# The MLP's two products by one level of Strassen's algorithm, with the hidden factors passing through DRAM

## The chip, the cores and the metric

One Trainium2 chip (trn2), one of its cores. The metric is device microseconds (us) for one execution of the whole program, lower is better. A core has a matrix engine (PE), which multiplies a stationary 128 x 128 block by a moving block of up to 512 columns into one of eight PSUM banks; a vector engine (DVE); a scalar engine (ACT); GpSimd (POOL); and a queue (SP) that issues DMAs. ACT issues DMAs as well. Every engine takes its instructions in the order in which they stand in its own queue.

## The reference

One layer of a hybrid block over 2048 latent tokens of width 1024 with 256 context tokens. The token mixer (Fourier mixing, a state-space layer and neighbourhood attention) is not touched here. What is touched is the second sub-layer:

```python
def sqrelu_mlp(h, w1, w2):
    return jnp.square(jax.nn.relu(h @ w1)) @ w2

h2 = modulate(rmsnorm(x, g_norm2[i]), sh2, sc2)
x = x + gt2 * sqrelu_mlp(h2, w_ff1[i], w_ff2[i])     # w_ff1 1024 x 4096, w_ff2 4096 x 1024
return rmsnorm(x, g_final)
```

## The kernel before, in words

The tail of the kernel is `merge_mlp`. It runs twice, over the tokens 1024 to 2047 and then 0 to 1023. Each half has three stages. `merged` makes the gated sum of the three branches. `projected` multiplies it by the output projection, adds the residual, and norms and transposes the result. `mlp` does the rest. Ahead of it stand the projections and the attention, which the change leaves as they are.

Every product is made to nearly float32 accuracy from factors that are each split in two float32r parts, high and low: `mm3` issues three matmuls (high by high, low by high, high by low; L176 to L178) for each pair of 128 x 128 and 128 x 512 blocks. A split is a copy on ACT (the high part, L169) and a subtraction on DVE (the low part, L173).

In `mlp`, 16 rounds each take two column blocks of 128 of the hidden layer. A round loads the weights, splits them, makes the hidden block for both blocks of 512 tokens (eight contraction blocks, 24 matmuls each), takes relu and square on ACT (L1366, L1367), splits the result, and multiplies by the rows of `w_ff2`. That is accumulated in SBUF: L1392 on DVE adds the PSUM bank into `x2`. The last round also norms and stores the output (L1394 to L1400). Over both halves there are 6144 matmuls of 512 columns.

All SBUF pages of these stages come from tagged rings: A1, X, W, R, T in one pool, A2, B1, B2 in another. A ring's next page waits for its earlier user. PSUM has banks g (2), t (2), s (3) and o (1). The program is written stage by stage, and a scheduler decides ahead of time how the instructions interleave on each engine; on the chip that order is fixed.

Of the kernel before, what the change touches and what calls it, by code (L numbers as in the profile page):

```python
# [20 lines left out]
P = 128  # L21
D = 1024
# [18 lines left out]
def constants():  # L41
    """Tables that depend on the shapes alone: DFT matrices and the column window."""
# [57 lines left out]
def block_kernel(ctx: ExitStack, tc: tile.TileContext, I, out, C, stages=None, taps=None):  # L100
# [32 lines left out]
    cd = dram.tile([8, P, 2, 2, P], F32, name="cd")  # L133
    scratch = dict(ud=ud, zd=zd, qd=qd, kd=kd, vd=vd, gd=gd, fad=fad, sbd=sbd, ncd=ncd, rid=rid)
# [10 lines left out]
    # ------------------------------------------------------------------ vectors  # L145
# [20 lines left out]
    # ------------------------------------------------------------------ helpers  # L166
# [8 lines left out]
    def mm3(out_, lh, ll, rh, rl, first, last):  # L175
        nc.tensor.matmul(out_, lh, rh, start=first, stop=False)  # L176
        nc.tensor.matmul(out_, lh, rl, start=False, stop=False)  # L177
        nc.tensor.matmul(out_, ll, rh, start=False, stop=last)  # L178
# [27 lines left out]
    # ------------------------------------------------------------------ modulation, first part  # L206
# [22 lines left out]
    def modulation(m1, c):  # L229
        """shift and scale of column tile c, for x and ctx"""  # L230
# [32 lines left out]
    # ------------------------------------------------------------------ phase A: u f k v q  # L263
# [14 lines left out]
    def products(wh, wl, blocks, kouter):  # L278
        """the blocks of tokens and their products with a unit of weights"""
# [67 lines left out]
    def gate(n, hx, half, kouter=False):  # L347
        """gd holds tanh(logit / 2)"""
# [6 lines left out]
    with pool("pa", side="right") as pa:  # L355
# [41 lines left out]
        # ------------------------------------------------------------------ modulation, second part  # L397
# [30 lines left out]
        # ---- relative-position tables: rows of rpd hold the bias at qc - kc + 63, 64 copies each, so that  # L428
        # a step of a row less one entry is a step of kc
# [37 lines left out]
    # ---- gated linear unit; sbd holds 4 * sb  # L467
# [143 lines left out]
def exp_dve(nc, sb, x, out, tag):  # L611
    """out = exp(x), to float32 accuracy; x is [P, n] and is overwritten."""
# [20 lines left out]
def sincos_dve(nc, sb, x, sn, cs):  # L633
    """sn, cs = sin(x), cos(x); x is [P, n] and is overwritten."""
# [24 lines left out]
    # odd quadrants exchange sine and cosine  # L659
# [12 lines left out]
def cmul(v, tmp, ore, oim, ar, ai, br, bi):  # L672
    """(ore, oim) = a * b, elementwise; the outputs may not be the inputs."""
# [8 lines left out]
def cmul_neg(v, tmp, ore, oim, ar, ai, br, nbi):  # L682
    """(ore, -oim) = a * b, for nbi = -im(b)."""
# [8 lines left out]
def s5_prep(g):  # L692
    """What depends on the parameters alone, into DRAM: lmd, ld (driving), kmd (chunk), cd (read-out).
    Three parts, so that other work can be placed between them."""
# [3 lines left out]
    with pool("s5") as sp:  # L698
        # ---- parameters: states (g2, p) on partitions, (direction, pair) along the free axis
# [4 lines left out]
        with pool("s5p") as pp:  # L704
# [27 lines left out]
            # (lbar - 1) / lam  # L732
# [18 lines left out]
            # powers of lbar, 0..8  # L751
# [6 lines left out]
            # powers of lbar**8, 1..16  # L758
# [9 lines left out]
            # bbar  # L768
# [6 lines left out]
            # c with states on partitions  # L775
# [22 lines left out]
        with pool("s5x") as sx:  # L798
# [9 lines left out]
            # X = lbar**i * bbar, in the order of the powers that the driving products need  # L808
# [9 lines left out]
            # read-out, rows (re, -im) of the states  # L818
# [46 lines left out]
def s5(g):  # L865
# [5 lines left out]
    with pool("s5", side="right") as sp:  # L871
# [4 lines left out]
        def load_u(sp, a, n):  # L876
            """the tokens of pairs a..a+n: (t, c) on partitions, (pair, h) and chunks along the free axis"""
# [12 lines left out]
        # ---- driving term of every chunk of 8 tokens  # L890
        with pool("s5x", side="right") as sx, pool("s5k", side="right") as sk:
# [21 lines left out]
            # ---- products within a chunk: both directions and the skip  # L913
# [63 lines left out]
        # ---- read-out  # L977
# [50 lines left out]
def attention(g):  # L1028
# [6 lines left out]
    with pool("at", side="right") as at:  # L1035
# [4 lines left out]
        def table(h):  # L1040
# [7 lines left out]
            # rows 4..28 see their own window of rows alone  # L1048
# [24 lines left out]
        def rows_of(a, q):  # L1073
            """query rows of quarter q that see a key row of tile a: all are contiguous"""
# [140 lines left out]
def merge_mlp(g):  # L1215
# [3 lines left out]
    G = 2  # L1219
# [7 lines left out]
    def small(shape=(P, NB), dt=F32):  # L1227
        return page("T", shape, dt)
# [9 lines left out]
    def branches(t0, b, br):  # L1238
        """the branches' outputs, transposed; the attention's rows are divided by their sums here"""
# [22 lines left out]
    def merged(t0, br):  # L1262
        """gated merge, transposed: m[d, tokens]"""
        parts = ((0, 2, "w_br_a"), (2, 4, "w_br_b"), (4, 8, "w_br_c"))
        mp, got = {}, {}
        for d, b in [(0, 0), (1, 0), (0, 1), (1, 1)] + [(d, b) for d in range(2, KT) for b in range(2)]:
# [15 lines left out]
            for i, (k0, k1, _) in enumerate(parts):  # L1282
# [4 lines left out]
                if i == 1:  # L1287
                    # the tokens of the second branch are in the order (t, c) for c * 8 + t
# [14 lines left out]
    def projected(t0, mp):  # L1303
        """output projection and residual, tokens on partitions; then the second norm"""
        x2, h2 = [], {}
        for n in range(2):
# [12 lines left out]
            for a in range(8):  # L1319
# [10 lines left out]
                if n == 1 and a % 4 == 3:  # L1330
                    b = a // 4
                    tiles = []
                    for aa in range(4 * b, 4 * b + 4):
                        r = rms(x2[aa])
                        xn = page("B1", (P, D), F32)
                        v.tensor_scalar(xn, x2[aa], r, None, op0=OP.mult)
                        tiles.append(xn)
                    for k in range(KT):
                        pt = psum("t")
                        for i, t in enumerate(tiles):  # L1340
                            nc.tensor.transpose(pt[:, i * P:(i + 1) * P], t[:, k * P:(k + 1) * P], ident)
                        tmp = small()
                        nc.scalar.activation(tmp, pt, AF.Identity, scale=g.a2[:, k:k + 1], bias=g.b2[:, k:k + 1])
                        p = page("A2" if b else "A1")
                        v.tensor_copy(p[:, 0], tmp)
                        v.tensor_tensor(p[:, 1], tmp, f32(p)[:, 0], op=OP.subtract)
                        h2[b, k] = p
        return x2, h2

    def mlp(t0, x2, h2, ahead):  # L1350
        """the MLP, the residual and the final norm; ahead() is placed before the last products"""
        for f0 in range(0, FF // P, G):
            hid, w2s = [], []
            for f in range(f0, f0 + G):
                raw = page("R", (P, KT, P), F32)
                nc.sync.dma_start(raw, I["w_ff1"][0, :, f * P:(f + 1) * P].rearrange("(k p) c -> p k c", p=P))
                wh = page("W", (P, KT, P))
                wl = page("W", (P, KT, P))
                g.splitw(raw, wh, wl)
                hb = []  # L1360
                for b in range(2):
                    pt = psum("g")
                    for k in range(KT):
# [79 lines left out]
```

## Time and profile before

| | |
|---|---|
| median of 3 runs | 3287.97 us (3285.66 to 3290.91) |
| span of the profiled execution | 3297.3 us |
| PE busy | 3182.4 us, 97% of the span |
| PE weight loads (beside the matmuls) | 78% |
| DVE, ACT, POOL busy | 59%, 36%, 20% |
| first `mlp` stage | about 1674 to 2395 us |
| second `mlp` stage | about 2577 to 3288 us |

The profiled execution is 9.3 us longer than the median. Matmuls are pipelined: the duration of one (0.39 us) is not what it adds to the time; the spacing of their starts is.

### The profile page before, as it was taken

How to read it: one execution, taken by the hardware profiler on the slowest of the kernel's cores; microseconds unless marked ns; L12 is line 12 of the kernel's file. 1: busy time of each engine (PE TensorE's matmuls, PEld its weight loads, DVE VectorE, ACT ScalarE, POOL GpSimd, SP SyncE). 2: the span in 40 equal slices, each digit the busy share in tenths (PEclk: the TensorE clock that was granted, in tenths of full speed). 3: DMA queues.
4: the chain of work that ended last, by engine and by line, in shares of the span. 5: the costliest groups of instructions: out<-in, count | busy, mean ns of one | idle time of the engine just before them, and what ended most of it. 6: DMA issues, size and time to landing. Idle time of an engine off the chain costs nothing.

```text
span 3297.3 us, 40319 instructions
## 1 busy us (share of the span) xinstructions
PE 3182.4 (97%) x14742; PEld 2585.7 (78%) x14742; DVE 1956.6 (59%) x3466; ACT 1185.8 (36%) x2153; POOL 664.9 (20%) x709
## 2 busy tenths in 40 slices
PE   8999787999999999999999999999999999999998
PEld 4887666788887788887788888888877888888887
DVE  6534379965888888847554444444575544444444
ACT  4242143364665556532232222222422322222222
POOL 0510124202565655524100000000151000000000
PEclk9999888999999999999999999999999999999999
DMA  6668863465436443266311111111473111111111
GB/s 207 200 202 247 207 164 98 140 190 174 115 114 207 115 119 111 84 184 193 118 39 51 51 52 51 40 50 45 121 255 108 40 45 51 52 52 49 41 48 61
DMA packets 394173, 370.26 MB, mean 112 GB/s; under 512 B 90688, under 2 KB 308943, under 8 KB 393591
## 3 DMA queue, kind: packets, MB, share of 16 engines
q1 hardware_dynamic: 310150, 294.80, 30.7%
q10 hardware_dynamic: 83248, 71.97, 7.1%
q8 instruction: 116, 1.90, 0.2%
q0 software_dynamic: 576, 0.92, 0.1%
q14 instruction: 83, 0.67, 0.1%
HBM read 282.79 MB, written 89.01 MB: 113 GB/s over the span
## 4 chain that ended last, share of the span: by engine, by line
PE 73%; DVE 6%; DMA 4%; ACT 0%; issue 0%; SPq 0%; POOL 0%; ACTq 0%; DVEq 0%; POOLq 0%
PE ps_g L176 13%; PE ps_g L177 13%; PE ps_g L178 13%; PE ps_s L178 5%; PE ps_s L176 5%; PE ps_s L177 5%; PE ps_t L176 4%; PE ps_t L178 4%; PE ps_t L177 4%; PE ps_s L1107 3%; PE ps_o L1160 1%; PE ps_o L1159 1%; PE ps_o L1163 1%; DMA pgR<-in_w_out_dram 1%; DVE Sx L975 1%; DVE tq L974 1%
## 5 line engine op out<-in xcount | busy, mean ns | idle before, releaser
L176 PE MATMUL ps_g<-pgA,pgW 128*128 128x512 f32 x1088 | 429.8, 395 | 2.4 <-DVE pgX L1292 1.5
L177 PE MATMUL ps_g<-pgA,pgW 128*128 128x512 f32 x1088 | 428.4, 394 | 0.0
L178 PE MATMUL ps_g<-pgA,pgW 128*128 128x512 f32 x1088 | 427.6, 393 | 0.0
L176 PE MATMUL ps_g<-hxh,whi 128*128 128x512 f32 x1024 | 408.0, 399 | 11.6 <-ACT ev L352 6.2
L178 PE MATMUL ps_g<-hxh,wlo 128*128 128x512 f32 x1024 | 406.4, 397 | 0.0
L177 PE MATMUL ps_g<-hxl,whi 128*128 128x512 f32 x1024 | 405.9, 396 | 0.0
L1392 DVE TENSOR_TENSOR pgX<-ps_t,pgX 128x512 f32<-128x512 f32 x256 | 176.1, 688 | 283.8 <-PE ps_t L178 283.7
L1235 POOL TENSOR_TENSOR st<-st,half_neg 128x1 f32<-128x1 f32 x32 | 22.2, 695 | 1573.4 <-DVE st L1234 1573.4
L1157 POOL TENSOR_TENSOR pl<-st,ph 128x512 fp32r<-128x512 f32 (+7 forms) x256 | 269.9, 1069 | 166.0 <-ACT ph L1155 154.7
L169 ACT ACTIVATE pgB<-pgR 128x1024 fp32r<-128x1024 f32 x64 | 68.0, 1063 | 647.1 <-PE ps_t L177 625.8
L176 PEld LDWEIGHTS ps_g<-pgA,pgW 128*128 128x128 f32 x1088 | 204.1, 188 | 49.9 <-DVE pgX L1292 1.9
L173 DVE TENSOR_TENSOR pgW<-pgR,pgW 128x1024 fp32r<-128x1024 f32 x80 | 106.9, 1336 | 228.4 <-ACT pgW L169 228.2
L178 PEld LDWEIGHTS ps_g<-pgA,pgW 128*128 128x128 f32 x1088 | 204.1, 188 | 47.8
L177 PEld LDWEIGHTS ps_g<-pgA,pgW 128*128 128x128 f32 x1088 | 204.1, 188 | 46.5
L176 PEld LDWEIGHTS ps_g<-hxh,whi 128*128 128x128 f32 x1024 | 195.5, 191 | 53.0 <-ACT ev L352 7.4
L177 PEld LDWEIGHTS ps_g<-hxl,whi 128*128 128x128 f32 x1024 | 195.6, 191 | 38.7 <-issue 0.5
L178 PEld LDWEIGHTS ps_g<-hxh,wlo 128*128 128x128 f32 x1024 | 195.3, 191 | 37.9
L1392 DVE TENSOR_TENSOR pgX<-ps_s,pgX 128x512 f32<-128x512 f32 x256 | 176.0, 688 | 68.1 <-PE ps_s L178 67.9
L178 PE MATMUL ps_t<-pgB,pgB 128*128 128x512 f32 x512 | 200.3, 391 | 0.0
L178 PE MATMUL ps_s<-pgB,pgB 128*128 128x512 f32 x512 | 200.2, 391 | 0.0
L176 PE MATMUL ps_t<-pgB,pgB 128*128 128x512 f32 x512 | 200.1, 391 | 0.0
L177 PE MATMUL ps_t<-pgB,pgB 128*128 128x512 f32 x512 | 199.8, 390 | 0.0
(439 smaller groups left out, 6828.8 us busy)
## 6 DMA issues: line engine op xcount, KB each, us to landing
pgR<-in_w_ff_dram SPq DMA_DIRECT2D x128, 512.0 KB
wraw<-in_w_in_dram SPq DMA_DIRECT2D x80, 512.0 KB
gd<-ev ACTq DMA_DIRECT2D x96, 256.0 KB
pgX<-gd SPq DMA_DIRECT2D x48, 512.0 KB
wm<-in_w_mod_dram SPq DMA_DIRECT2D x64, 256.0 KB
qs<-qd SPq DMA_DIRECT2D x128, 128.0 KB
wm<-in_w_mod_dram SPq DMA_DIRECT2D x16, 512.0 KB
xt<-in_x_dram SPq DMA_DIRECT2D x16, 512.0 KB
```

The source lines that it names most:

```text
L169: nc.scalar.activation(hi, raw, AF.Copy)
L173: e.tensor_tensor(lo, raw, f32(hi), op=OP.subtract)
L176: nc.tensor.matmul(out_, lh, rh, start=first, stop=False)
L177: nc.tensor.matmul(out_, lh, rl, start=False, stop=False)
L178: nc.tensor.matmul(out_, ll, rh, start=False, stop=last)
L974: v.tensor_tensor(tq, lm[l][:, h], car[c][:, h], op=OP.mult)
L975: v.tensor_tensor(dst[o][:, h], dst[o][:, h], tq, op=op)
L1107: nc.tensor.matmul(o, kk[:, j * P:(j + 1) * P], qs[:, i, p0:p1], start=i == 0, stop=i == 1)
L1157: e.tensor_tensor(pl[:, c0:c1], st[:, c0:c1], f32(ph)[:, c0:c1], op=OP.subtract)
L1159: nc.tensor.matmul(po[0:65, p0:p1], vh[:, j], ph[:, p0:p1], start=n == 0, stop=False)
L1160: last = nc.tensor.matmul(po[0:64, p0:p1], vl[:, j], ph[:, p0:p1], start=False, stop=False)
L1392: v.tensor_tensor(x2[a][:, cs], pt, x2[a][:, cs], op=OP.add)
```

## The change

One level of Strassen's algorithm (the form with seven block products and shared sums) replaces both products of the MLP. Each factor is cut into 2 x 2 blocks; seven products of sums and differences of blocks stand in for eight. Three PSUM accumulators are used per product (`CHAIN`): a bank is read after one block product and then accumulated on by the next.

The stages are taken apart. `projected` now also makes the seven token factors (28 splits, `factor`, and 4 kinds of differences, half of them on POOL) and stores the residual to DRAM (`x2d`). `hidden` makes all hidden blocks: 16 blocks q of 256 hidden columns, each of seven products of 12 matmuls. `prepare(q)` loads `w_ff1` (2 x 512 KB on SP) and makes four sums and differences on DVE (L1397 to L1400). `finish` (L1407 to L1435) takes the blocks out of PSUM, applies relu and square, makes three sums and differences on POOL that the second product will need, and writes seven float32 factors to DRAM (`hcd`) with five DMAs. `mlp` then reads them back: four quarters q, each of seven products of 48 matmuls over four banks, with both factors split anew; a quarter loads 8 x 512 KB of `w_ff2` and 14 x 512 KB of `hcd`. The result lies in eight SBUF pages `y`, and the gate `gt2`, the residual (read back from `x2d`) and the final norm come at the very end, where before `gt2` had been multiplied into the weights. Over both halves there are 5376 matmuls of 512 columns.

```diff
+    x2d = dram.tile([2, KT, P, D], F32, name="x2d")
+    hcd = [dram.tile([7, 16, P, NB], F32, name=f"hcd{t}") for t in range(2)]
...
+        def factor(j, k, src, tag):
+            p = page(tag)
+            nc.scalar.activation(p[:, 0], src, AF.Copy)
+            v.tensor_tensor(p[:, 1], src, f32(p)[:, 0], op=OP.subtract)
+            TW[j, k] = p
...
+                        if b == 0:
+                            factor(0, kk, blk[0, kk][:, 0], "A1")
+                            factor(1, kk, blk[0, kk][:, 1], "A1")
+                        else:
+                            t1, t2 = small(), small()
+                            nc.gpsimd.tensor_tensor(t1, blk[1, kk][:, 0], blk[0, kk][:, 0], op=OP.subtract)
+                            v.tensor_tensor(t2, blk[1, kk][:, 1], t1, op=OP.subtract)
+                            factor(2, kk, t2, "A2")
+                            factor(3, kk, t1, "A2")
+        for kk in range(4):
+            t1, t2 = small(), small()
+            nc.gpsimd.tensor_tensor(t1, blk[1, kk][:, 1], blk[1, kk][:, 0], op=OP.subtract)
+            factor(4, kk, t1, "B1")
+            factor(5, kk, blk[1, kk][:, 1], "B1")
+            nc.gpsimd.tensor_tensor(t2, blk[0, kk][:, 1], blk[0, kk][:, 0], op=OP.subtract)
+            nc.gpsimd.tensor_tensor(t2, t2, t1, op=OP.subtract)
+            factor(6, kk, t2, "B2")
...
+    CHAIN = ((0, True), (1, True), (0, False), (2, True), (0, False), (2, False), (0, False))
+    def hidden(t0, TW):
...
...
+        for q, j in steps:
+            if j == 0:
+                srcs[q], bank[q], cs[q] = prepare(q), {}, {}
+            b, new = CHAIN[j]
+            p = page("W", (P, 2, 4, P))
+            nc.scalar.activation(p[:, 0], srcs[q][j], AF.Copy)
+            v.tensor_tensor(p[:, 1], srcs[q][j], f32(p)[:, 0], op=OP.subtract)
+            if new:
+                bank[q][b] = psum("sgt"[b])
+            pt = bank[q][b]
+            for k in range(4):
+                t = TW[j, k]
+                mm3(pt, p[:, 0, k], p[:, 1, k], t[:, 0], t[:, 1], new and k == 0, k == 3, not new)
+            finish(q, j, pt, cs[q])
...
+    def mlp(t0, ahead):
+        for q in range(4):
...
+            for j in range(7):
+                L = split(hs, "B1")
+                R = split(src[j], "A2")
+                    for k in range(4):
+                        for i in range(4):
+                            product(i, k)
+                    for i in range(4):
+                        evict(i)
+                if last and j >= 5:
+                    for a in range(4 * (j - 5), 4 * (j - 4)):
+                        nc.sync.dma_start(xr, g.x2d[t0 // HALF, a])
+                        v.tensor_tensor(y[a], y[a], gt2, op=OP.mult)
+                        v.tensor_tensor(y[a], y[a], xr, op=OP.add)
+                        r = rms(y[a])
+                        v.scalar_tensor_tensor(y[a], y[a], r, gf, op0=OP.mult, op1=OP.mult)
+                        nc.scalar.dma_start(out[0, t0 + a * P:t0 + (a + 1) * P, :], y[a])
```

Up to the end of the first `projected` every engine's queue holds the same instructions in the same order as before. From there the queues differ. Three places follow.

The first is POOL's queue at the end of the first `projected`. Before, the four reciprocal roots of the last four token tiles (L1235) are all that stands there until the end of the half:

```order
L1235 TENSOR_TENSOR st_16871<-st_16871,half_neg_91 128x1
L1235 TENSOR_TENSOR st_16878<-st_16878,half_neg_91 128x1
L1235 TENSOR_TENSOR st_16885<-st_16885,half_neg_91 128x1
L1235 TENSOR_TENSOR st_16892<-st_16892,half_neg_91 128x1
L1235 TENSOR_TENSOR st_21429<-st_21429,half_neg_91 128x1
```

Now the sixteen differences of the token factors stand behind them, four of L1362 and then these twelve (pgT are the differences, pgB2 the transposed token blocks; the first of L1426 is already the hidden stage's):

```order
L1368 TENSOR_TENSOR pgT_16997<-pgB2_16905 128x512
L1371 TENSOR_TENSOR pgT_16998<-pgB2_16693 128x512
L1368 TENSOR_TENSOR pgT_17011<-pgB2_16928 128x512
L1371 TENSOR_TENSOR pgT_17012<-pgB2_16712 128x512
L1368 TENSOR_TENSOR pgT_17025<-pgB2_16951 128x512
L1372 TENSOR_TENSOR pgT_16998<-pgT_16998,pgT_16997 128x512
L1371 TENSOR_TENSOR pgT_17026<-pgB2_16731 128x512
L1368 TENSOR_TENSOR pgT_17039<-pgB2_16974 128x512
L1372 TENSOR_TENSOR pgT_17012<-pgT_17012,pgT_17011 128x512
L1371 TENSOR_TENSOR pgT_17040<-pgB2_16750 128x512
L1372 TENSOR_TENSOR pgT_17026<-pgT_17026,pgT_17025 128x512
L1372 TENSOR_TENSOR pgT_17040<-pgT_17040,pgT_17039 128x512
```

POOL had nothing of this size there; now it has a queue of sixteen operations of 128 x 512, the last of which makes the last part of the seventh token factor (`pgT_17040`).

The second is DVE's queue at the same place, from the split that reads that last difference on (pgW are the split weights; 17149 and 17166 are those of the products j = 2 and j = 3 of the first block, the fifth and sixth products that PE's queue holds):

```order
L1313 TENSOR_TENSOR pgB2_17050<-pgT_17040,pgB2_17050 128x512
L1398 TENSOR_TENSOR pgB2_17057<-pgB2_17057,pgX_17053 128x512
L1398 TENSOR_TENSOR pgB2_17105<-pgB2_17105,pgX_17101 128x512
L1400 TENSOR_TENSOR pgB2_17058<-pgX_17055,pgB2_17057 128x512
L1400 TENSOR_TENSOR pgB2_17106<-pgX_17103,pgB2_17105 128x512
L1448 TENSOR_TENSOR pgW_17149<-pgB2_17057,pgW_17149 128x512
L1448 TENSOR_TENSOR pgW_17166<-pgB2_17057,pgW_17166 128x512
```

Before, the casts and subtractions of the transposed tokens (L1345, L1346) stood between the split weights of that place. Now the weights of the fifth product to run stand behind the split of the seventh token factor.

The third is DVE's queue at the end of the program. Before, a residual add (L1392) and a final scaling (L1399) alternate:

```order
L1399 SCALAR_TENSOR_TENSOR pgX_22394<-pgX_22394,st_27404,pgB1_27316 128x1024
L1392 TENSOR_TENSOR pgX_22422<-ps_t_27418,pgX_22422 128x512
L1392 TENSOR_TENSOR pgX_22450<-ps_t_27441,pgX_22450 128x512
L1392 TENSOR_TENSOR pgX_22506<-ps_s_27479,pgX_22506 128x512
L1234 TENSOR_SCALAR st_27427<-st_27427 128x1
```

Now each of the eight pages passes DVE three more times (L1546 gate, L1547 residual, L1549 scaling), all of it behind the sixth of the last quarter's seven products. This is where the last pages' sums (L1529) stand:

```order
L1546 TENSOR_TENSOR pgX_25615<-pgX_25615,gt2_15527 128x1024
L1236 TENSOR_SCALAR st_27741<-st_27741 128x1
L1529 TENSOR_TENSOR pgX_25617<-ps_s_27291,pgX_25617 128x512
L1547 TENSOR_TENSOR pgX_25614<-pgX_25614,pgB2_27758 128x1024
L1549 SCALAR_TENSOR_TENSOR pgX_25611<-pgX_25611,st_27730,pgR_27267 128x1024
L1546 TENSOR_TENSOR pgX_25616<-pgX_25616,gt2_15527 128x1024
L1529 TENSOR_TENSOR pgX_25618<-ps_o_27292,pgX_25618 128x512
```

The gate and the residual moved from the weights and from the start value of the sum to a chain at the end.

## Rows read from the trace of the kernel before

**Rows 1.** The page's head: the span, and the busy time of each engine.
```profile
span 3297.3 us, 40319 instructions
PE 3182.4 (97%) x14742; PEld 2585.7 (78%) x14742; DVE 1956.6 (59%) x3466; ACT 1185.8 (36%) x2153; POOL 664.9 (20%) x709
```

**Rows 2.** Busy us of each engine (instructions) by stretch, granted clock, DMA share, GB/s.
```profile
core 0: us, PE busy (x) PEld busy (x) DVE busy (x) ACT busy (x) POOL busy (x), PEclk, DMA share, GB/s
1800.00:1900.00 100.00, 100.00 (x437) 81.66 (x437) 46.45 (x60) 22.75 (x32) 0.00 (x0) 1.00 0.14 42
2400.00:2500.00 100.00, 93.06 (x391) 73.51 (x390) 78.23 (x94) 25.25 (x37) 48.95 (x32) 0.98 0.71 234
```

**Rows 3.** PE's timeline around the end of the first projection: start, duration, what.
```profile
1674.07 0.40 PE L178 MATMUL ps_s<-pgA,pgB 128*128 128x512 f32 x1
1674.31 0.39 PE L176 MATMUL ps_g<-pgA,pgW 128*128 128x512 f32 x1
1675.00 1.04 PE L1341 MATMUL ps_t<-ident,pgB 128*128 128x128 f32 x8
```

**Rows 4.** As rows 2, the hand-over to the MLP and the program's end.
```profile
1674.00:1690.00 16.00, 15.71 (x90) 12.95 (x89) 12.18 (x24) 10.15 (x15) 0.55 (x1) 1.00 0.11 33
3287.70:3297.30 9.60, 0.00 (x0) 0.00 (x0) 5.08 (x7) 1.75 (x4) 2.06 (x3) 0.61 0.55 218
```

**Rows 5.** As rows 2, between the two halves.
```profile
2390.00:2416.00 26.00, 19.41 (x73) 14.24 (x72) 20.87 (x30) 6.53 (x10) 8.72 (x7) 0.93 0.96 330
2409.00:2412.00 3.00, 3.00 (x8) 2.40 (x9) 2.30 (x4) 1.27 (x2) 1.45 (x1) 0.53 1.02 408
```

**Rows 6.** ACT's timeline: evictions of the last transposed tokens.
```profile
1681.19 3.11 ACT L1343 ACTIVATE pgT<-ps_t,b,a 128x512 f32<-128x512 f32 x4 [3.06 <-PE ps_t L1341]
```

**Rows 7.** POOL's element-wise operations by source line: shortest, median and longest ns.
```profile
L1294 POOL TENSOR_TENSOR pgX<-pgX x64: 1274/1610/2284, 1497.0 to 2490.7; 128x512 f32<-128x512 f32 x64
L1397 POOL TENSOR_TENSOR pgX<-pgX,pgB x4: 2400/2632/3319, 2372.0 to 2385.1; 128x1024 f32<-128x1024 f32 x4
```

**Rows 8.** DVE's groups in the first MLP: count, busy us, mean ns, idle before.
```profile
L1392 DVE TENSOR_TENSOR pgX<-ps_t,pgX 128x512 f32<-128x512 f32 x126 | 86.7, 688 | 141.5 <-PE ps_t L178 141.5
L173 DVE TENSOR_TENSOR pgB<-pgT,pgB 128x512 fp32r<-128x512 f32 x64 | 44.1, 690 | 39.0 <-ACT pgB L169 38.9
L173 DVE TENSOR_TENSOR pgB<-pgR,pgB 128x1024 fp32r<-128x1024 f32 x32 | 39.1, 1220 | 17.8 <-ACT pgB L169 17.8
```

**Rows 9.** ACT's groups in the first MLP, columns as in rows 8.
```profile
L169 ACT ACTIVATE pgB<-pgT 128x512 fp32r<-128x512 f32 x63 | 39.6, 631 | 1.5
L1366 ACT ACTIVATE pgT<-ps_g 128x512 f32<-128x512 f32 x62 | 36.5, 591 | 77.2 <-PE ps_g L178 77.2
L169 ACT ACTIVATE pgB<-pgR 128x1024 fp32r<-128x1024 f32 x29 | 30.8, 1063 | 321.1 <-PE ps_t L177 312.9 <-DVE pgR L1374 8.1
```

**Rows 10.** ACT's issue of an output DMA, by source line, ns as in rows 7.
```profile
L1400 ACTq DMA_DIRECT2D out_dram<-pgX x16: 338/338/361, 2375.4 to 3293.4; - x16
```

**Rows 11.** DVE's timeline while POOL works.
```profile
2414.33 2.35 DVE L173 TENSOR_TENSOR pgW<-pgR,pgW 128x1024 fp32r<-128x1024 f32 x1 [0.17 <-ACT pgW L169]
2417.80 0.67 DVE L1292 SCALAR_TENSOR_TENSOR pgX<-pgX,ps_t 128x512 f32<-128x512 f32 x1
```

**Rows 12.** POOL's timeline at the same time.
```profile
2414.31 1.29 POOL L1294 TENSOR_TENSOR pgX<-pgX 128x512 f32<-128x512 f32 x1 [3.86 <-DVE pgX L1292]
2417.36 6.04 POOL L1294 TENSOR_TENSOR pgX<-pgX 128x512 f32<-128x512 f32 x4 [1.76 <-DVE pgX L1290]
```

**Rows 13.** The final scaling, group in columns as in rows 8.
```profile
L1399 DVE SCALAR_TENSOR_TENSOR pgX<-pgX,st,pgB 128x1024 f32<-128x1024 f32 x12 | 15.3, 1279 | 1.5 <-POOL st L1235 1.4
```

**Rows 14.** The chain that ended last, in order of time: a load, a store.
```profile
1551.52 5.80 DMA pgR<-in_w_out_dram
2400.40 7.65 DMA out_dram<-pgX
```

**Rows 15.** The same chain at the program's end.
```profile
3290.87 1.28 DVE pgX L1399
3292.15 1.20 DVEq L1439
```

More of the change, by code (lines that the diff above doesn't have):

```diff
@@ L173, in splitw, with mm3 @@
         e.tensor_tensor(lo, raw, f32(hi), op=OP.subtract)
[L175 to L178, printed above, removed]
+    def mm3(out_, lh, ll, rh, rl, first, last, more=False):
+        nc.tensor.matmul(out_, lh, rh, start=first, stop=False, skip_group_check=more)
+        nc.tensor.matmul(out_, lh, rl, start=False, stop=False, skip_group_check=more)
+        nc.tensor.matmul(out_, ll, rh, start=False, stop=last, skip_group_check=more)
     def rms_tile(sb, xt, n):
@@ L1303, in projected @@
     def projected(t0, mp):
-        x2, h2 = [], {}
+        x2, TW, blk = [], {}, {}
+        def factor(j, k, src, tag):
[3 more added lines that the diff above has]
+            TW[j, k] = p
         for n in range(2):
@@ L1336, in projected @@
                         v.tensor_scalar(xn, x2[aa], r, None, op0=OP.mult)
+                        nc.scalar.dma_start(g.x2d[t0 // HALF, aa], x2[aa])
                         tiles.append(xn)
[L1338 to L1363, printed above, removed]
-                        mm3(pt, wh[:, k], wl[:, k], h2[b, k][:, 0], h2[b, k][:, 1], k == 0, k == KT - 1)
-                    r = small()
-                    nc.scalar.activation(r, pt, AF.Relu)
-                    nc.scalar.activation(r, r, AF.Square)
-                    p = page("B1")
-                    g.splitw(r, p[:, 0], p[:, 1])
-                    hb.append(p)
-                hid.append(hb)
-                raw = page("R", (P, D), F32)
-                nc.sync.dma_start(raw, I["w_ff2"][0, f * P:(f + 1) * P, :])
-                v.tensor_tensor(raw, raw, gt2, op=OP.mult)
-                vh = page("B2", (P, D))
-                vl = page("B2", (P, D))
-                g.splitw(raw, vh, vl)
-                w2s.append((vh, vl))
-            last = f0 + G == FF // P
@@ new lines, in projected @@
+        for kk in range(4):
+            t1, t2 = small(), small()
[5 more added lines that the diff above has]
+            factor(6, kk, t2, "B2")
+        return TW
+    ORDER = (0, 1, 2, 3, 4, 5, 6)
+    CHAIN = ((0, True), (1, True), (0, False), (2, True), (0, False), (2, False), (0, False))
@@ new lines, in mlp, with split @@
+    def mlp(t0, ahead):
+        hcd = g.hcd[t0 // HALF]
+        y = [page("X", (P, D), F32) for _ in range(8)]
+        halves = [slice(n * NB, (n + 1) * NB) for n in range(2)]
+        def split(src, tag):
+            out = []
+            for s in src:
+                h, l = page(tag), page(tag)
+                nc.scalar.activation(h, s, AF.Copy)
+                v.tensor_tensor(l, s, f32(h), op=OP.subtract)
+                out.append((h, l))
+            return out
+        for q in range(4):
+            w = {}
+            for kk, n in ((0, 0), (1, 0), (0, 1), (1, 1)):
+                w[kk, n] = []
+                for h in range(2):
+                    r = page("A1", dt=F32)
+                    f0 = (8 * q + 4 * h) * P
+                    nc.sync.dma_start(r, I["w_ff2"][0, f0:f0 + 4 * P, halves[n]].rearrange(
+                        "(a k p) c -> k p a c", k=2, p=P)[kk])
+                    w[kk, n].append(r)
+            src = {0: w[0, 0], 1: w[1, 0]}
+            last = q == 3
@@ L1380, in mlp @@
             if last:
[L1381 removed]
+                gf = page("R", (P, D), F32)
                 nc.sync.dma_start(gf, bap(I["g_final"], 0, [[0, P], [1, D]]))
[L1383 to L1400 removed]
+            bank = {}
@@ L1415, in merge_mlp @@
         mp = merged(t0, br)
-        x2, h2 = projected(t0, mp)
-        mlp(t0, x2, h2, f)
+        hidden(t0, projected(t0, mp))
+        mlp(t0, f)
 _INS = ["x", "c", "ctx", "c_ctx", "w_mod", "b_mod", "g_norm1", "g_norm2", "w_in", "w_br_a", "w_br_b", "w_br_c",
```

119 lines of the change are left out of this document (100 added, 19 removed).

## Prediction

> **What bounds the kernel now.** I read the page's head first [rows 1]: PE is busy for 97% of the span, no other engine for more than 59%. Then the busy time by stretch [rows 2]. Inside an MLP stage PE is full, the granted clock is at its upper level (2.4 GHz), and 437 matmuls start in 100 us: one per 0.2288 us. That spacing, not the 0.40 us of a single record [rows 3], is the price of a matmul. The DMA share in the same row is 0.14 (42 GB/s), so memory has room. ACT's idle time in this stage ends on PE's matmul [rows 9], and so does DVE's at its residual add [rows 8]. So in the MLP PE is the limit, and fewer matmuls save time, as long as the other engines keep up with the new order. The two places where PE pauses today are the change of halves and the end [rows 4, 5].
>
> **What is removed.** 6144 matmuls become 5376, all of 128 x 512. 768 x 0.2288 = **175.7 us**. That is the only gain. All the rest of the change is new work on DVE, ACT, POOL and DMA, and I ask of each stage whether it hides behind PE.
>
> **A. From projection to hidden stage, twice.** Before, PE stays busy here: 15.71 of 16.00 us, in the first row of [rows 4]. Now the token factors stand between. The last projection matmul starts at 1674.07 [rows 3], and the queues are the same up to there. Behind it PE has 40 transposes, 1.04 us for eight [rows 3], 5.2 us in all, and the 48 matmuls of the hidden stage's first four products, 11.0 us. It runs dry at about 1690.3. The fifth product needs a split weight (`pgW_17149`) that DVE's queue holds behind the split of POOL's last difference. So POOL sets the time.
>
> POOL's first difference needs a second evicted block: ACT evicts from 1681.19, 0.78 us each [rows 6], so it starts at 1682.8. The next three follow as ACT goes on, which now evicts two blocks (2 x 0.78) and makes two copies (2 x 0.63, [rows 9]) for each: 2.8 us apart. Twelve more need only POOL. Its price for 128 x 512 lies between 1.27 and 2.28 us, median 1.61 [rows 7]. I take 1.7, above the median, because DVE works beside all of them. The fourth ends at 1682.8 + 3 x 2.8 + 1.7 = 1692.9, the last at 1692.9 + 12 x 1.7 = 1713.3. Then come one copy on ACT (0.63) and six operations on DVE at 0.69 [rows 8], 4.8 us together: 1718.1. PE stands 27.8 us. Behind a pause it also starts at the lower clock: with 0.53 granted it made 8 matmuls in 3.00 us [rows 5], which is 3.00 - 8 x 0.2288 = 1.2 us lost. 29 per half, **58 us** in all. With 1.27 the end is at 1707.7 (19 us per half), with 2.28 at 1725.6 (37): 38 to 74.
>
> Does DVE pace it instead? In the same stretch its queue holds some 32 operations of 128 x 512. At 0.69 that is 22 us from 1684 on and hides behind POOL. But with both operands in SBUF a DVE subtraction of 128 x 1024 took 2.35 us while POOL was at work [rows 11, 12], against 1.22 on the average [rows 8]; an add whose source is a PSUM bank took 0.67 beside POOL, nothing lost. If nothing of the two overlapped, 16 x 1.27 on POOL plus 32 x 0.69 on DVE, 42.4 us from 1682.8, ends at 1725: 7 us later per half than the sum has. The Trainium skill ("SBUF — State Buffer", section "Who interferes with whom") states just that as a rule: DVE's second port pair is GpSimd's, under an exclusive lock, and the loser stands still. By that rule A would be 72 instead of 58; the trace agrees for the single operation (2.35 against 1.22), but a whole stretch of this mix no run here shows.
>
> **Hidden stage, steady.** A block of seven products is 84 matmuls, 19.2 us of PE. Beside it ACT has 18 operations at about 0.62 [rows 9] and 5 DMA issues at 0.34 [rows 10], 12.9 us; DVE 14 x 0.69 = 9.7; POOL 4 x 1.7 = 6.8. Seven factors of 256 KB written and 1 MB of weights read per block come to some 150 GB/s, where this chip reached 330 [rows 5]. Nothing reaches 19.2. The order leaves each eviction and the copy behind it 1 to 2 us. Cost: nothing in the sum; a rival below.
>
> **B. From hidden to the second product, twice.** The pages for `w_ff2` come free only in the last block, and so do the loads: five pages of 512 KB at 1.6 (330 GB/s) to 2.6 us plus a latency of some 3.4 us, the rest of a whole load of 5.80 us [rows 14] without 2.4 of transfer, then three DVE operations of 1.22: 15 to 20 us, against 13.75 us of matmuls still queued (60 of them). About 3 per half, **6 us** (0 to 16).
>
> **Second product, steady.** A product is 48 matmuls, 11.0 us. ACT has at most 6.6; DVE four splits at 1.22 and four adds at 0.69, 7.6. Per quarter: PE 76.9, DVE 58, POOL 4 x 2.63 [rows 7] = 10.5. Even if DVE and POOL excluded each other, 68.8 is below 76.9. 22 loads of 512 KB per quarter are again some 150 GB/s. PE stays the bound. For late pages at the quarters and in the hidden stage together I take **5 us** (0 to 20).
>
> **C. Between the halves.** When PE ends the sixth product of the first half's last quarter, DVE's queue holds eight sums (0.69), eight gates and eight residual adds (1.22 each), eight scalings (1.28, [rows 13]), and then 15 operations of the next half's merge (0.68) for which PE waits: 5.5 + 9.8 + 9.8 + 10.2 + 10.3 = 45.6 us. PE has 132 matmuls in that time, 30.2 us. It stands 15.4, plus 1.2 for the clock. Today it stands 26.00 - 19.41 = 6.6 us here [rows 5], with the same 1.2. **9 us** more (4 to 18).
>
> **D. The end.** After the sixth product DVE has the same 35.3 us without the merge, PE only 11.0 us. DVE ends some 24 us behind PE. Today 9.6 us pass from PE's last matmul to the end [rows 4]; the final scaling starts at 3290.87 and takes 1.28, and then 5.1 us of output and drain follow [rows 4, 15]. 24.3 + about 3.9 (the last issue and store follow at once) against 9.6 gives some 18; I take **17.5 us** (14 to 25).
>
> **Sum.** 175.7 - 58 - 6 - 5 - 9 - 17.5 = 80. The profiled execution goes from 3297.3 to about 3217. It is 9.3 us above the median of the runs, and I take that difference to stay: 3287.97 - 80 = 3208. With A between my estimate and the case in which POOL and DVE exclude each other I lean a little to that side: **3210 us**. The gain is less than half of what the fewer matmuls give, because at the seams between the stages (A to D) PE is left without work.
>
> **Rivals.** *Slower: the hidden stage's hand-over.* ACT issues the DMA of two sums (L1435) in its queue between evictions, and that issue waits for POOL's L1434. If POOL is late, ACT's next evictions and weight copies are, and PE with them. There are 32 blocks: a stall of 2.5 us in each (80 / 32) takes the whole gain back, and with 1 to 2 us of room that asks for a POOL some 4 us late; at 4 us per block the time is 3208 + 128 = 3336. For it speaks POOL's spread up to 2.28 us [rows 7]; against it that POOL has four operations in 19.2 us. 10%.
>
> *Strict exclusion at A*, as worked out above: 2 x 7 us more, 3222. It needs no new mechanism, and lies in the forecast's range.
>
> *A short hand-over.* If the differences run at 1.27 throughout, and the evictions ahead of them come a few us sooner, PE stands 15 per half: 3208 - 28 = 3180. For it speak the shortest of [rows 7]; against it DVE's work beside them. 14%.
>
> *The gain does not come in the second product.* If all of DVE's splits ran at 2.35 us as in [rows 11], a product would have 4 x 2.35 + 4 x 0.69 = 12.2 us of DVE against 11.0 of PE: 85 instead of 76.9 per quarter, 66 us over eight, 3274. It decides from a mean split of 2.06 us on; below that PE paces. Against it: POOL works only a seventh of a quarter. 8%.
>
> **How the numbers follow.** A measurement of this kernel tells some 0.2% (6.6 us) from no change. The forecast, with strict exclusion in it, holds 68%, from 3190 to 3240; the short hand-over 14%, the second product without gain 8%, the slow hidden stage 10%. The range 3168 to 3262 takes in the forecast, the short hand-over and the milder half of the second product's case, and so the bounds of A (38 to 74) with those of B to D. Faster 0.86: the forecast, the short hand-over and most of the second product's case; same 0.04, slower 0.10, the hidden rival and mishaps of its size.
>
> **What would show it.** Right: 5376 matmuls in the MLP at 0.227 to 0.234 spacing; two holes of PE of 20 to 37 us just behind each `projected`, with POOL busy throughout and the split of `pgT_17040`'s kind at their end; holes of a few us at hidden to `mlp`; DVE alone at work for some 24 us at the end, and PE short of some 15 us between the halves; inside the stages no PE wait of weight. Wrong: a spacing of matmuls above 0.235 in the stages, waits of PE on ACT's or DVE's splits in each block, or holes that end on a DMA.

## The result, and the profile after

The changed kernel takes 3205.53 us (median), the kernel before 3289.44 beside it: a ratio of 0.9749, 95% interval 0.9733 to 0.9764. One of its four runs took 7602 us, at a mean granted clock of 0.396 where the others had 0.968 to 0.970, and the ratio leaves it out. Predicted were 3210, from 3168 to 3262. A second measurement of the same kernel gave 0.9761, so two measurements of one kernel differ by some 4 us.

The page's head, as in [rows 1]:

```profile
span 3202.9 us, 40653 instructions
PE 3008.8 (94%) x13974; PEld 2442.2 (76%) x13974; DVE 2159.7 (67%) x3566; ACT 1423.3 (44%) x2525; POOL 987.1 (31%) x897
```

The busy time by stretch, columns as in [rows 2]: the hand-over to the hidden stage (two rows), the hidden stage, the second product, the change of halves, and what follows the last matmul:

```profile
1674.00:1690.00 16.00, 5.35 (x33) 3.79 (x31) 12.11 (x11) 10.50 (x18) 11.77 (x8) 0.73 0.00 0
1690.00:1720.00 30.00, 7.03 (x18) 5.37 (x19) 27.38 (x31) 10.55 (x20) 12.63 (x8) 0.52 0.16 52
1800.00:1900.00 100.00, 100.00 (x432) 80.70 (x431) 52.27 (x72) 54.16 (x93) 27.15 (x21) 1.00 0.43 147
2200.00:2300.00 100.00, 100.00 (x443) 82.79 (x442) 83.94 (x89) 41.55 (x45) 12.57 (x4) 1.00 0.53 161
2330.00:2360.00 30.00, 19.71 (x66) 14.15 (x65) 29.39 (x36) 7.45 (x12) 16.96 (x10) 0.77 0.70 234
3178.16:3202.90 24.74, 0.00 (x0) 0.00 (x0) 20.39 (x26) 5.75 (x10) 9.56 (x7) 0.60 0.43 170
```

PE is full inside both stages and empty at the seams, where DVE is the full engine (27.38 of 30, 29.39 of 30). PE's waits between the first projection and the change of halves are two short lists (the engine, the tile and the line that wait; what released them; us in total, how often, the longest); the first is of 1676 to 1720, the second of 1720 to 2330:

```profile
PE ps_s L179 <- ACT pgW L1447: 33.0, 1, 33.0
PE ps_t L1354 <- ACT pgB L1355: 0.6, 2, 0.4
```

```profile
PE ps_s L179 <- ACT pgT L1407: 0.5, 1, 0.5
```

One wait of 33 us, and 0.5 us in the 610 us after it. The end of the first projection and the restart of PE in its timeline:

```profile
1662.73 0.40 PE L181 MATMUL ps_s<-pgA,pgB 128*128 128x512 f32 x1
...
1712.97 0.79 PE L179 MATMUL ps_s<-pgA,pgW 128*128 128x512 f32 x1 [32.96 <-ACT pgW L1447]
1713.56 0.63 PE L180 MATMUL ps_s<-pgA,pgW 128*128 128x512 f32 x1
```

The first of these rows answers to 1674.07 in [rows 3]: the same matmul starts 11.3 us earlier here, though the queues are the same up to it. So 11.3 us of the profiled execution of before were lost ahead of everything that the change touches. From that matmul on, before needed 3297.3 - 1674.07 = 1623.2 us, the changed kernel 3202.9 - 1662.73 = 1540.2: 83.1 us less, where the medians differ by 83.9. In what follows traces are compared from there, and the stretch from this matmul to the end is called the part behind the projection.

POOL's timeline in the hole:

```profile
1682.55 1.71 POOL L1368 TENSOR_TENSOR pgT<-pgB 128x512 f32<-128x512 f32 x1
1694.25 1.70 POOL L1368 TENSOR_TENSOR pgT<-pgB 128x512 f32<-128x512 f32 x1
1695.92 1.71 POOL L1372 TENSOR_TENSOR pgT<-pgT 128x512 f32<-128x512 f32 x1
1697.58 1.71 POOL L1371 TENSOR_TENSOR pgT<-pgB 128x512 f32<-128x512 f32 x1
1699.25 3.38 POOL L1372 TENSOR_TENSOR pgT<-pgT 128x512 f32<-128x512 f32 x2
```

And DVE's, in the same microseconds and after POOL's end, with ACT's copy of the fifth product's weights at the end:

```profile
1694.76 1.74 DVE L1313 TENSOR_TENSOR pgB<-pgT,pgB 128x512 fp32r<-128x512 f32 x1
1696.43 1.75 DVE L1313 TENSOR_TENSOR pgB<-pgB,pgB 128x512 fp32r<-128x512 f32 x1
1698.09 1.75 DVE L1313 TENSOR_TENSOR pgB<-pgT,pgB 128x512 fp32r<-128x512 f32 x1
...
1704.44 0.69 DVE L1313 TENSOR_TENSOR pgB<-pgT,pgB 128x512 fp32r<-128x512 f32 x1
1705.05 0.69 DVE L1313 TENSOR_TENSOR pgB<-pgB,pgB 128x512 fp32r<-128x512 f32 x1
...
1710.96 0.69 DVE L1313 TENSOR_TENSOR pgB<-pgT,pgB 128x512 fp32r<-128x512 f32 x1
1711.57 1.29 DVE L1398 TENSOR_TENSOR pgB<-pgB,pgX 128x512 f32<-128x512 f32 x2
1712.29 2.19 ACT L1447 ACTIVATE pgW<-pgB 128x512 fp32r<-128x512 f32 x4 [2.81 <-DVE pgB L1398]
```

While POOL works, both engines start one operation every 1.67 us, in step. When POOL ends (1702.63), DVE's splits start every 0.60 us. DVE comes to the split of the last difference only at 1710.96, 8.3 us after POOL has made it (1.6 us of that it waits for ACT); the weights' sum (L1398), ACT's copy of it and PE follow within 2.0 us.

### The profile page after: what moved, and what is told of

It reads as the page before. It is cut to its first block, busy times and chain, and to the rows that moved or that the text cites. A ratio compares the mean times of both kernels' runs of the same rounds, so it can differ in the third digit from the quotient of the medians.

```text
span 3202.9 us, 40653 instructions
## 1 busy us (share of the span) xinstructions
PE 3008.8 (94%) x13974; PEld 2442.2 (76%) x13974; DVE 2159.7 (67%) x3566; ACT 1423.3 (44%) x2525; POOL 987.1 (31%) x897
## 4 chain that ended last, share of the span: by engine, by line
PE 69%; DVE 9%; DMA 4%; ACT 1%; issue 1%; SPq 0%; POOL 0%; ACTq 0%; DVEq 0%; POOLq 0%
PE ps_g L180 8%; PE ps_g L181 8%; PE ps_g L179 8%; PE ps_s L179 7%; PE ps_s L181 7%; PE ps_s L180 7%; PE ps_t L179 4%; PE ps_t L180 4%; PE ps_t L181 4%; PE ps_s L1110 3%; PE ps_o L1163 2%; PE ps_o L1162 2%; PE ps_o L1166 1%; DMA pgR<-in_w_out_dram 1%; DVE tq L977 1%
## 5 line engine op out<-in xcount | busy, mean ns | idle before, releaser
L1468 ACT ACTIVATE pgB<-pgB 128x1024 fp32r<-128x1024 f32 x112 | 118.7, 1060 | 278.9 <-PE ps_o L180 135.5
L1469 DVE TENSOR_TENSOR pgB<-pgB,pgB 128x1024 fp32r<-128x1024 f32 x112 | 151.4, 1353 | 95.6 <-ACT pgB L1468 95.6
L179 PE MATMUL ps_s<-pgA,pgW 128*128 128x512 f32 x320 | 129.0, 403 | 66.8 <-ACT pgW L1447 65.9
L1132 DVE TENSOR_TENSOR mx<-mx,st 128x384 f32<-128x384 f32 (+2 forms) x224 | 184.1, 822 | 4.0
L180 PE MATMUL ps_s<-pgA,pgB 128*128 128x512 f32 x464 | 181.1, 390 | 0.0
L179 PE MATMUL ps_s<-pgA,pgB 128*128 128x512 f32 x464 | 181.1, 390 | 0.0
L181 PE MATMUL ps_s<-pgA,pgB 128*128 128x512 f32 x464 | 180.9, 390 | 0.0
L1426 POOL TENSOR_TENSOR pgR<-pgT 128x512 f32<-128x512 f32 x32 | 43.1, 1348 | 378.3 <-ACT pgT L1416 378.3
L1151 ACT ACTIVATE st<-st 128x512 f32<-128x512 f32 (+7 forms) x288 | 129.3, 494 | 66.4 <-DVE st L1150 59.2
L1158 ACT ACTIVATE ph<-st 128x512 fp32r<-128x512 f32 (+7 forms) x288 | 135.5, 497 | 34.8 <-PE ps_o L1163 20.9
L1296 POOL TENSOR_TENSOR pgX<-pgX 128x512 f32<-128x512 f32 x64 | 98.0, 1538 | 142.3 <-DMA gd<-ev 61.9
L180 PE MATMUL ps_g<-pgA,pgB 128*128 128x512 f32 x352 | 137.8, 392 | 1.9 <-DVE pgA L175 1.9
L1150 DVE TENSOR_TENSOR st<-st,ps_t 128x512 f32<-128x512 f32 (+7 forms) x288 | 132.1, 523 | 8.9 <-PE ps_t L1142 8.8
```

What stands on the lines that cost most here:

```text
L179: nc.tensor.matmul(out_, lh, rh, start=first, stop=False, skip_group_check=more)
L180: nc.tensor.matmul(out_, lh, rl, start=False, stop=False, skip_group_check=more)
L181: nc.tensor.matmul(out_, ll, rh, start=False, stop=last, skip_group_check=more)
L1132: v.tensor_tensor(M[:, c0:c1], M[:, c0:c1], st[:, c0:c1], op=OP.max)
L1150: v.tensor_tensor(st[:, c0:c1], st[:, c0:c1], mb[:, c0:c1], op=OP.subtract)
L1151: nc.scalar.activation(st[:, c0:c1], st[:, c0:c1], AF.Exp)
```

## The experiments

All ratios are to the kernel before, measured beside each; the changed kernel's are 0.9749 and 0.9761, so 0.001 is 3.3 us. A difference of medians below some 6 us says little. The part behind the projection tells more: it is 1540.2 us in the changed kernel's first trace and 1541.2 in its second. The start of that matmul moves far more, from 1660.6 to 1674.1 us over all twelve traces, and it moves ahead of the merge: from the merge's first matmul to this one it is 179.6 to 180.2 us in every trace but one (182.8, with the split weights in the other pool).

**The sixteen differences on DVE.** The token factors need twenty differences, of which sixteen are on POOL (the section on the change has half of them there) and four on DVE already (L1363). At L1362, L1368, L1371 and L1372:

```diff
-            nc.gpsimd.tensor_tensor(t1, ...
+            v.tensor_tensor(t1, ...
```

> All sixteen differences of the token factors go from POOL to DVE; nothing else changes. Theory 1 (at the hand-over POOL and DVE take turns: a DVE split and a POOL difference together cost 1.67 us there, against 0.60 for a DVE split alone): DVE has 43 operations instead of 31, but at 0.60 us, so PE's pause after each projection shrinks from 33 us to about 24, and the time goes from 3205.5 to about 3187 (3180 to 3195). Theory 2 (the number of operations alone counts, no taking turns): DVE gains 12 operations behind the last transposes and loses nothing, the pause grows by about 7 us per half, 3220. Theory 3 (the pause ends on the weights of the first blocks, not on the factors): no change, 3205.

Measured: 3185.5, ratio 0.9696 (0.9678 to 0.9714). PE's wait there, as in the list above:

```profile
PE ps_s L179 <- ACT pgW L1447: 24.5, 1, 24.5
```

Theory 1's number, 24, is met; the part behind the projection is 19.4 us shorter (1520.7 against 1540.2). From 1682.6 on DVE's operations start 0.60 us apart, the splits (L1313) too, which had started 1.67 apart beside POOL:

```profile
1695.24 0.68 DVE L1313 TENSOR_TENSOR pgB<-pgB,pgB 128x512 fp32r<-128x512 f32 x1
1695.84 0.68 DVE L1313 TENSOR_TENSOR pgB<-pgT,pgB 128x512 fp32r<-128x512 f32 x1
```

Giving DVE twelve more operations in the hole made the hole shorter, because POOL beside it had cost DVE more time than the work that POOL did for it.

**The weights ahead of the later factors.** The loop that makes factors 5 to 7 is called from `hidden` before step 6; the four differences of the first token half (L1371) are made where that half's tokens are transposed, before the projection ends.

```diff
+        for n, (q, j) in enumerate(steps):
+            if n == 6:
+                TW["rest"]()
```

> The split weights of the fifth and sixth product stand ahead of the token factors 5 to 7, and four of the differences are made in the first half of the projection's tail; all stays on POOL. If the place in DVE's queue sets the pause (the weights wait behind 14 splits that the next products do not need), PE restarts when the third and fourth factor are there, some 18 us earlier, runs 24 matmuls (5.6 us) and waits again for the fifth to seventh: the pauses shrink from 33 to about 18 to 22 us per half, 3205.5 goes to about 3180 (3172 to 3190). If the sum of the work of DVE and POOL sets it whatever the order, the pause is filled only by the 24 matmuls: about 3194.

Measured: 3189.47, ratio 0.9703 (0.9686 to 0.972), some 17 us better than the changed kernel. PE's waits from 1676 to 1720:

```profile
PE ps_s L179 <- ACT pgW L1454: 12.7, 1, 12.7
PE ps_t L1354 <- ACT pgB L1355: 3.8, 1, 3.8
PE ps_s L181 <- DVE pgW L1455: 3.2, 1, 3.2
PE ps_t L1354 <- DVE pgB L1346: 0.9, 1, 0.9
```

That is 20.6 us instead of 33.6, within the 18 to 22 of the forecast. The projection's last matmul starts at 1673.10 in this trace and PE restarts at 1707.58: 34.5 us behind it instead of 50.2, so 15.8 us earlier where 18 were forecast. The part behind the projection is 22.5 us shorter (1517.7). The forecast of 3180 asked for 25, the case in which the sum of the work counts (3194) for 12. So the trace speaks for the place in the queue; the median, at 3189, lies between the two cases and does not part them. DVE's operations still took 1.75 us beside POOL.

**Gate and residual ahead of the sum.** The gate is multiplied into `w_ff2` after its load, `x2d` is loaded into `y` as the start value, L1546 and L1547 go.

```diff
+                    v.tensor_tensor(r, r, gt2[:, None, halves[n]].to_broadcast([P, 2, NB]), op=OP.mult)
...
-                        v.tensor_tensor(y[a], y[a], gt2, op=OP.mult)
-                        v.tensor_tensor(y[a], y[a], xr, op=OP.add)
```

> The gate is multiplied into the second product's weights again (8 DVE operations of 1.22 us per quarter), and the residual is the start value of the sum, as before the change; the chain at the end loses 16 of its 32 long operations, and the first writes of the sum go from ACT to DVE. If the price of the end is DVE's queue behind the sixth product: the tail after the last matmul goes from 24.7 us to about 9, and the pause between the halves from 12 to 7 or less; the weights reach PE some 3 us later at the start of each second product (6 us in all): 3205.5 goes to about 3190 (3183 to 3197). Rival: DVE has 68 us of work for 77 us of PE in each quarter, falls behind at the quarters' boundaries and gives the gain back: 3200 to 3215.

Measured: 3192.04, ratio 0.9712 (0.9695 to 0.9728). By stretch, what follows the last matmul, and the second product:

```profile
3179.72:3188.40 8.68, 0.00 (x1) 0.00 (x0) 3.47 (x6) 1.23 (x3) 1.09 (x2) 0.61 0.50 201
2200.00:2300.00 100.00, 100.00 (x443) 82.86 (x442) 87.23 (x95) 42.47 (x45) 13.52 (x4) 1.00 0.43 132
```

The tail is 8.7 us instead of 24.74, the wait of 9.3 us between the halves is gone, and the first product of each half waits 3.4 us for the multiplied weights. DVE is at 87% of the second product and PE stays full. Behind the projection the trace is 19.2 us shorter, where the forecast had 15; the medians show 14.

**The split weights in the other pool.** `page` takes the ring W from `ml` instead of `mr`.

> The ring of split weights of the hidden stage lies in the other pool, at other addresses; no instruction changes. In the changed kernel matmuls follow each other at 0.2315 us in the hidden stage and at 0.2258 in the second product. If the spacing depends on whether both operands lie in the same pool (0.227) or in two (0.2333), five of the seven products become the closer kind and two the wider, 0.2288 on the mean: 2688 x 0.0027 = 7 us less, 3198. If it does not: 3205.

Measured: 3207.68, ratio 0.9755 (0.9736 to 0.9773): no change. But the hidden stage's row has 439 matmuls in 100 us instead of 432, and the part behind the projection is 8.3 us shorter:

```profile
1800.00:1900.00 100.00, 100.00 (x439) 82.18 (x438) 53.35 (x74) 54.87 (x95) 26.53 (x20) 1.00 0.44 149
```

Ahead of it the first merged product waited 7.3 us for a DMA, and the merge with the projection took 2.9 us longer:

```profile
1490.13 0.80 PE L179 MATMUL ps_g<-pgA,pgW 128*128 128x512 f32 x1 [7.34 <-DMA pgT<-rid]
```

The spacing moved as expected (0.2278 on the mean, 0.2288 forecast), the time did not. Product by product the theory holds: with the moving factor in B1 or B2 the mean distance of two starts goes from 0.2334 us (operands in two pools) to 0.2269 (in one), and in the bank `ps_g`, whose moving factor lies in A1, from 0.2287 (one pool) to 0.2335 (two). Whether the new wait belongs to the edit, which moves the merge's pages too, stays open.

**The hidden factors written twice.** Each of the five DMAs of a block goes to a second place as well.

> The hidden stage writes each of its five DMAs per block a second time, to another place in DRAM (it computes the same); ACT issues ten instead of five, 14.6 us of ACT work in 19.2 us of PE, and the traffic of the stage rises from some 150 to some 245 GB/s. If the round trip through DRAM is hidden behind PE: same, 3205 (3200 to 3212). Rival (ACT's queue or the DMA queues have no room): each block loses up to the 1.7 us of the added issues, 32 x 1.7 = 54 us, 3260.

Measured: 3220.5, ratio 0.9799 (0.9781 to 0.9817), some 15 us slower. In the stage nothing moved:

```profile
1800.00:1900.00 100.00, 100.00 (x432) 80.77 (x431) 51.26 (x70) 52.73 (x92) 28.86 (x22) 1.00 0.68 237
```

Still 432 matmuls with the traffic at 237 GB/s. Most of the loss lies in the last block of each half, in the stretch in which the loads of the second product start. In the first half PE and ACT waited there:

```profile
PE ps_s L180 <- ACT pgT L1420: 4.8, 1, 4.8
ACT pgT L1428 <- DMA hc<-pgT: 9.5, 1, 9.5
```

ACT waits for a write of the second copy to be done; in the second half it is 10.0 us, and 5.3 for PE. So the round trip is hidden, and the seam behind it has less room than the stage. Neither theory had that. What holds the write up there was not tried.

**POOL's work in the hidden block doubled.** L1426, L1427, L1428 and L1434, the block's four sums and differences on POOL (the section on the change counts three), each run twice.

> The four sums and differences on POOL in each hidden block are each made twice (same result). ACT's issue of the last DMA of a block waits for the last of them, and behind it stand ACT's next copies. POOL has 13.4 us of work in a block of 19.2. The prediction's slower rival says a late POOL passes through ACT to PE: if POOL's six operations ahead of that issue now end after the point where ACT comes to it, PE waits 1 to 4 us per block, 32 to 130 us in all. If the order leaves room for a POOL that is some 5 us later: 3205, and PE's spacing in the stage stays at 432 matmuls per 100 us.

Measured: 3259.16, ratio 0.9916 (0.99 to 0.9933): 53 us slower. PE waits in 24 of the 32 blocks, mostly 1.4 us: there two of its starts lie 1.83 us apart instead of 0.23. A block now takes 21.2 us instead of 19.5. A block of DVE's timeline, first of the changed kernel:

```profile
1864.81 0.69 DVE L1448 TENSOR_TENSOR pgW<-pgB,pgW 128x512 fp32r<-128x512 f32 x1 [5.12 <-ACT pgW L1447]
1865.54 0.69 DVE L1397 TENSOR_TENSOR pgB<-pgX 128x512 f32<-128x512 f32 x1
1866.15 0.68 DVE L1448 TENSOR_TENSOR pgW<-pgB,pgW 128x512 fp32r<-128x512 f32 x1
1866.75 1.78 DVE L1398 TENSOR_TENSOR pgB<-pgB,pgX 128x512 f32<-128x512 f32 x1
1868.46 0.68 DVE L1414 TENSOR_TENSOR pgT<-pgT,ps_g 128x512 f32<-128x512 f32 x1
```

And of the experiment, at the same place of a block:

```profile
1860.39 1.27 DVE L1448 TENSOR_TENSOR pgW<-pgB,pgW 128x512 fp32r<-128x512 f32 x1 [5.11 <-ACT pgW L1447]
1861.70 1.67 DVE L1397 TENSOR_TENSOR pgB<-pgX 128x512 f32<-128x512 f32 x1
1863.29 1.78 DVE L1448 TENSOR_TENSOR pgW<-pgB,pgW 128x512 fp32r<-128x512 f32 x1
1864.99 1.78 DVE L1398 TENSOR_TENSOR pgB<-pgB,pgX 128x512 f32<-128x512 f32 x1
1866.69 0.67 DVE L1414 TENSOR_TENSOR pgT<-pgT,ps_g 128x512 f32<-128x512 f32 x1
```

From the first split to the add of L1414 it is 3.65 us in the one and 6.30 in the other. ACT's relu waits for that add, ACT's next eviction stands behind the relu, and PE waits for that. Of 2.65 us, some 1.0 were room and 1.7 reached PE.

**The same, with the two waiting DMAs on SP.** L1429 and L1435 are issued by `nc.sync`.

> As the kernel with the doubled POOL operations of the hidden stage (55 us more than the changed kernel), but the two DMAs that wait for POOL are issued by SP instead of ACT, so nothing in ACT's queue waits for POOL any more. Theory 1 (the prediction's rival: ACT is stuck at the issue that waits for POOL, and PE behind it): the 55 us go away, 3205 with PE at 432 matmuls per 100 us. Theory 2 (the traces so far: DVE's splits and sums take 1.3 to 1.8 us instead of 0.6 while POOL works, so DVE's add of the fifth product is late, then ACT, then PE): the time stays at about 3259, with the same wait of some 1.8 us in each block.

Measured: 3250.17, ratio 0.9888 (0.9867 to 0.9909). PE's waits in 100 us of the hidden stage, which read the same with the issue on ACT:

```profile
PE ps_s L179 <- ACT pgT L1407: 7.2, 5, 1.4
```

Theory 2: taking POOL out of ACT's queue gave back at most 9 us of 53, a difference that the two intervals do not settle; in the part behind the projection it is 5.7 us of 47.7 (1582.2 against 1587.9). What is left is DVE slowed by POOL: from the first split to the add of L1414 it is 6.25 us here, as against 6.30.

**Two repairs together.** The differences on DVE, and the gate in the weights.

> Only the sixteen differences on DVE, and the gate in the weights with the residual as start value. Alone the first shortened the trace behind the first projection's transposes by 19.5 us, the second by 19.3. If they are separate costs, they add: 3166 (3160 to 3172). If they share a cause (DVE), the second gives back part of the first: 3175 or more.

Measured: 3173.25, ratio 0.9653 (0.9631 to 0.9675). Against the changed kernel (0.9755, the mean of its two) that is 33 us; alone they gave 19 and 14. The median lies between the two cases (3160 to 3172, and 3175 or more). The part behind the projection decides: it is 37.9 us shorter (1502.3), against 19.4 + 19.2 = 38.6 for the two alone. They are separate costs and add.

**All three.** As above, with the weights ahead of the later factors.

> Together: the differences of the token factors on DVE (but the four early ones of the first token half, on POOL), the weights of the fifth and sixth product ahead of the later factors, the gate in the weights and the residual as start value. If the two pauses and the end are separate costs that DVE's queue sets, the gains add: at least that of the two without the new place of the weights (39 us, 3166), and another 5 to 10 us per half because PE has 24 matmuls to run while DVE makes the last factors: 3146 to 3158. If the sum of DVE's work is all that counts there, the new place of the weights adds nothing: 3166.

Measured: 3150.09, ratio 0.9578 (0.9556 to 0.9601). This beats both kernels: 4.2% below the kernel before. PE's three longest waits from the first projection to the change of halves:

```profile
PE ps_s L179 <- ACT pgW L1454: 6.9, 1, 6.9
PE ps_s L181 <- DVE pgW L1455: 5.0, 1, 5.0
PE ps_g L180 <- DVE pgA L1478: 3.4, 1, 3.4
```

The one wait of 33 us has become two, 11.9 us together. Behind the projection the trace is 15.0 us shorter than with the two repairs (1487.3 against 1502.3), where the forecast had 10 to 20 more from the new place of the weights. Whether that place is worth more with POOL out of the way is not shown: by the medians it brought 25 us here and 17 with POOL beside it (the second experiment), by the traces 15 and 22.5.

**The changed kernel again.**

> The changed kernel itself once more, beside the others on the same chip: 0.975 of the kernel before, 3205; it tells how far two measurements of one kernel differ.

Measured: 3208.44, ratio 0.9761 (0.9737 to 0.9785).

## Why the prediction was right, and where its terms were off

The forecast of some 80 us was met (83.1 in the trace, 83.9 in the medians), by the mechanism that it named: the matmuls go, PE stays the bound inside both stages, and the seams take half of the gain. Its terms were less exact than its sum.

- **Saved, 175.7.** The spacing is 0.2315 us in the hidden stage (432 in 100 us) and 0.2257 in the second product (443), against 0.2288. Over 2688 matmuls each this is some +7 and -8 us: nothing in the sum.
- **A, 58 predicted, 71 measured.** This is the term that was mis-sized. From the projection's last matmul PE ran dry after 17.2 us (predicted 16.2), POOL was done after 39.9 (39.2), PE started again after 50.2 (44.0). POOL's queue was right to a microsecond, at 1.67 to 1.71 us per difference. What failed is the step "then come one copy on ACT and six operations on DVE, 4.8 us": DVE, held to POOL's pace, was 8.3 us behind when POOL ended, and from there to PE's restart it was 10.3 us. With the lower clock behind the pause (2.9 us in the first half, 1.7 in the second, 1.2 predicted) this is about 35 per half, where the text put the case of strict exclusion at 36. So the rival that lay inside the forecast came true, nearly. The Trainium skill's rule ("SBUF — State Buffer", section "Who interferes with whom"), an exclusive lock between the two engines' SBUF ports, gives the direction, and the experiment without POOL confirms it: the pause went from 33.0 to 24.5 us. The trace softens it: alone a DVE operation takes 0.60 us of its queue, and a POOL difference in the hidden stage 1.25, 1.85 together; in step they took 1.67. The term's lower bound was also worked out wrongly: with differences at 1.27 us it leaves out the 4.8 us that the upper bound includes, and should be 23 us per half and 47 in all, not 19 and 38.
- **Hidden stage, nothing predicted, nothing found.** PE waited 0.5 us in 610. The slower rival's path was wrong in kind: with POOL late it is DVE, not ACT's issue of the DMA, that carries the delay to PE. Its room of 1 to 2 us was about right (1.0), and its price real: twice the work on POOL took 53 us, nearly two thirds of the gain.
- **B, 6 predicted, 2 measured** (a wait of 0.5 us in the first half and 1.2 in the second, both for ACT's eviction and not for a load), and **late pages, 5 predicted, none found**. The loads of the next product, at 326 GB/s in 2000 to 2060, came in time.
- **C, 9 predicted, 7 measured.** Summed over the starts of PE's matmuls between the halves, 13.4 us are pauses and 3.1 the lower clock, against 7.4 and 2.1 before.
- **D, 17.5 predicted, 15.1 measured** (24.74 against the 9.6 of [rows 4]). The queue was the one named; its operations were priced by duration, 1.22, while they start 1.13 apart.

Together 71 + 2 + 7 + 15 = 95 of cost, against 95.5 predicted: A was 13 too low, and B to D with the late pages 13 too high. That the sum is within 3 us of the trace is this balance, which is luck: the mechanism was right, the sizes of A and of the rest were off in opposite directions.

## What to carry to other kernels

When an algorithm takes matmuls away, price the seams: the work that makes its new factors must have something of PE's to hide behind, and where a stage boundary leaves nothing, half of the gain goes there. Do not share element-wise work between DVE and POOL where DVE's operations read two SBUF operands and DVE is what PE waits for; here moving all of it to DVE shortened the pause from 33.0 to 24.5 us. Put into an in-order queue first what the next product needs, and gate weights early rather than results at the end of everything.

## What the runs showed that was not expected

- DVE and POOL in step at 1.67 us per pair: POOL's 128 x 512 difference went from 1.29 to 1.71 us and DVE's split from 0.69 to 1.75, while a DVE add with a PSUM operand kept 0.67 beside POOL (1866.69 in the experiment with POOL's work doubled).
- The spacing of matmuls of one shape differs with where their operands lie: 432 in 100 us with the split weights in one pool and most moving factors in the other, 439 with the weights moved, 443 in the second product, where both operands lie in one pool. In the hidden stages of both kernels it is 0.227 to 0.229 us where both operands lie in one pool, and 0.233 to 0.234 where they lie in two. What in the addresses of the two pools decides was not tried.
- After the pause of 33 us the first matmuls were at the lower clock: starts 0.43 us apart until 1719.08, then 0.23. Behind the second half's pause, equally long, it was 8 matmuls instead of 14.
